# MLA attention rows: one exponential base per row, unnormalised weights, and 1/sum applied to the 64x256 output

## The chip, the core and the metric

The kernel runs on one core of one Trainium2 chip. The metric is device time in microseconds (us) for one execution, on the slowest core in use (here the only one). A core has five engines that run side by side, each with its own queue of instructions executed in order: PE (matrix products), DVE (vector work), ACT (functions of one operand, casts, copies), POOL (a second, slower vector engine) and SP (here it only issues memory transfers). They wait for each other through semaphores. Products land in PSUM, eight banks of 128 x 512 fp32; everything else lies in SBUF or in the chip's memory.

## The reference, cut to what matters

One decoder layer over 16 meta tokens and 1024 real tokens: RMSNorm, an input projection, three groups of heads side by side (stick-breaking attention, a Mamba-2 scan, MLA attention), an output projection, and a SwiGLU feed-forward block. The change concerns MLA, 8 heads with a query and key of 96 and a value of 64:

```
scale = 1 / sqrt(96)
s = einsum(q, k) * scale                       # causal, 128 queries at a time
p = softmax(where(mask, s, -1e30), axis=-1)    # over at most 1040 keys
o = einsum(p, v)
```

## The kernel before, in words

Tokens lie feature-major (features on partitions). A product of fp32 accuracy is made of three passes on numbers split into a high and a low part (`whi`, `wlo`, `hnh`, `hnl`, `mhi`, `mlo`, `ph`, `pl`): high x high, low x high, high x low. `load_w` brings a 512 KB weight tile to `wraw` (one buffer), ACT casts it to `whi`, POOL makes `wlo` (two buffers each). `dense_fm` (L126) runs the three passes (L135 to L137) into one of two PSUM banks `d_ps`, which a callback then empties.

Program order gives each instruction a priority; the framework then lists, engine by engine and before anything runs, what stands where, so that products of a later part fill the turns in which attention waits. On the chip each engine keeps that fixed order.

The MLA stage runs over heads c = 0 to 7 (`mla_head`), and in a head over j = 0 to 3, a pair of blocks of 128 queries (i = 2j and 2j + 1). For each block `mla_row` works through one to three chunks of keys (`key_chunks`: one chunk for i = 0, 1, 2, two for i = 3 to 6, three for i = 7; so 112 chunks, 64 rows, 32 pairs in the stage). Per chunk: PE computes scores into one of three PSUM banks `sc_ps` (L901 to L903, and the causal mask by L906), DVE takes the chunk's maximum (L908) and turns it into a bias (L909), and ACT exponentiates from PSUM into `pr` with that bias and a sum beside it (L910). As each chunk has its own base, the chunks are afterwards brought to one: DVE takes the least bias (L918), ACT exponentiates the differences (L919), DVE forms the row's sum and a factor for each chunk (L920 to L923; L915 for a row of one chunk), and DVE multiplies the whole row by it (L926; in the last two heads POOL takes chunks 1 and 2).

`weighted_values` then transposes the rows by PE into PSUM (`ptm`, `ptg`, L310 to L321), ACT casts (`ph`, L305), DVE subtracts (`pl`, L306), PE multiplies with the values (`pv`, L295 to L299), ACT and DVE add the two halves of the result (`half` L329, `oT` L331: 64 partitions x 256 queries), and ACT issues the store to memory (`s_omla`, L337). The same function serves the stick-breaking heads.

The filling work beside MLA is first the gate's projection (`gate_units`: loads `gy` by SP, L475; `gy` times the gate by POOL, L479; result `go` by DVE, L481; 1/rms of the tokens at its end, `rc` and `dg`), then the first rows of the output projection (`out_rows`: loads `raw` from `s_osb` and `s_ossm`, L966; sums into `hT`, L986). After the stage comes `OutGroup`, the rest of the output projection (operands by L1012, L1015, L1018), which reads `s_omla` back (L1059).

Of the kernel before, what the change touches and what calls it, by code (L numbers as in the profile page):

```python
# [11 lines left out]
F32 = mybir.dt.float32  # L12
# [3 lines left out]
AF = mybir.ActivationFunctionType  # L16
ALU = mybir.AluOpType
# [6 lines left out]
SEQ = 1024  # L24
# [35 lines left out]
def tile_hybrid_block(ctx: ExitStack, tc: tile.TileContext, a: dict):  # L60
# [11 lines left out]
    # ------------------------------------------------------------------ pools  # L72
# [43 lines left out]
    # ------------------------------------------------------------- primitives  # L116
# [24 lines left out]
    def col_rsqrt(r, x, tmp):  # L141
        """r = x^-1/2: a seed within 4% from the float's bits, 0x5f3759df - (bits >> 1), then Newton."""
        ri, xi = r.bitcast(I32), x.bitcast(I32)
        dve.tensor_scalar(ri, xi, 1, None, ALU.arith_shift_right)
        dve.tensor_scalar(ri, ri, -1, 0x5F3759DF, ALU.mult, ALU.add)
        for _ in range(3):
            dve.tensor_tensor(tmp, r, r, op=ALU.mult)
            dve.scalar_tensor_tensor(tmp, x, -0.5, tmp, ALU.mult, ALU.mult)
            dve.scalar_tensor_tensor(r, tmp, 1.5, r, ALU.add, ALU.mult)

    def token_rstd(cols, ps, squares, blocks, width, bufs=1):
        """1/rms of each token as columns [token in block, block]: squares are feature-major
        tiles whose sum over partitions and tiles is the token's sum of squares."""
# [20 lines left out]
    def spread(diag, row, r, blocks, t0, wide=None, bufs=2):  # L174
        """row[:, t - t0] = r of token t, on every partition."""
# [24 lines left out]
    # ---------------------------------------------------- phase 0: hn^T hi/lo  # L200
# [10 lines left out]
    # tiles of tags that the second head pair needs later: raw weights, squares  # L211
# [23 lines left out]
    def first_operands(i):  # L235
        """gain * x of the chunk's tokens, not yet over their rms, as products' operands"""
# [120 lines left out]
    # ------- phase 1: stick-breaking attention; convolution and step sizes beside it  # L357
    def step_sizes():
# [14 lines left out]
        # dt = softplus(dt_raw + bias), token-major; log decay and its sum within each chunk  # L373
# [10 lines left out]
        # log1p(u) = 2 s (1 + s^2/3 + s^4/5 + ...), s = u / (2 + u) <= 1/3  # L384
# [16 lines left out]
        # exact three-way bfloat16 split of the head-major running sum  # L401
# [42 lines left out]
    def add_squares(u, tile_, c0, n):  # L444
        """squares of the tile's chunk onto the token's sums so far, in grow"""
# [11 lines left out]
    def latent_units(w, dst, mov, chunks, blocks):  # L457
        """a latent projection to memory; 1/rms of its tokens as columns [token in block, block]"""
# [11 lines left out]
    def gate_units():  # L470
        """s_ossm = y silu(z), and 1/rms of its tokens as columns"""
# [15 lines left out]
        # two units share the early tokens' turn: the last tokens' y comes last  # L487
# [8 lines left out]
    def sb_values(g, w, blocks, r=None, banks=None):  # L496
        """token-major values of head pairs 2g, 2g+1"""
# [54 lines left out]
    # the first projections take the operands before 1/rms is known and scale their results  # L552
# [89 lines left out]
    # ------------- phase 2: SSD; beside it MLA's operands and the gate's projection  # L642
    def spread_row(row, r, blocks, chunks):
        for c0, m in chunks:
# [3 lines left out]
            act.copy(row[:, c0 : c0 + m], ps[:, :m])  # L648
# [6 lines left out]
    with ExitStack() as st:  # L655
# [121 lines left out]
        def latent(src, nt, n, gain, r, blocks, chunks):  # L777
            """(c * gain) hi/lo tiles, and 1/rms of each token as a row"""
# [13 lines left out]
            spread_row(row, r, blocks, chunks)  # L792
# [11 lines left out]
        # shared rotated key  # L804
# [24 lines left out]
        cq_mov, cq_row = latent(s_cq, 3, SEQ, gq, cq_r, real, CH_REAL)  # L829
# [34 lines left out]
    scale = 1.0 / math.sqrt(96.0)  # L864
    with ExitStack() as st:
# [22 lines left out]
        def mla_row(proj, i, late):  # L888
# [7 lines left out]
            # columns: 0-2 -scale * chunk max, 3 the least of them, 4-6 sums, 7-9 factors  # L896
            sm = mr.tile([128, 12], F32, tag="sm", bufs=6, name="sm")
            for x, (c0, n) in enumerate(chunks):
# [5 lines left out]
                if last:  # L904
# [3 lines left out]
                dve.tensor_reduce(sm[:, x : x + 1], ps[:, :n], AX.X, ALU.max)  # L908
                dve.tensor_scalar(sm[:, x : x + 1], sm[:, x : x + 1], -scale, None, ALU.mult)  # L909
                act.activation(  # L910
                    pr[:, c0 : c0 + n], ps[:, :n], AF.Exp, scale=scale, bias=sm[:, x : x + 1],
                    accum_out=sm[:, 4 + x : 5 + x],
                )
            if nch == 1:
                dve.reciprocal(sm[:, 7:8], sm[:, 4:5])  # L915
            else:
                # chunk factor exp(chunk max - row max) / row sum
                dve.tensor_reduce(sm[:, 3:4], sm[:, 0:nch], AX.X, ALU.min)  # L918
                act.activation(sm[:, 7 : 7 + nch], sm[:, 0:nch], AF.Exp, scale=-1.0, bias=sm[:, 3:4])  # L919
                dve.tensor_tensor(sm[:, 4 : 4 + nch], sm[:, 4 : 4 + nch], sm[:, 7 : 7 + nch], op=ALU.mult)  # L920
                dve.tensor_reduce(sm[:, 10:11], sm[:, 4 : 4 + nch], AX.X, ALU.add)
                dve.reciprocal(sm[:, 10:11], sm[:, 10:11])
                dve.tensor_scalar(sm[:, 7 : 7 + nch], sm[:, 7 : 7 + nch], sm[:, 10:11], None, ALU.mult)  # L923
            for x, (c0, n) in enumerate(chunks):
                n = min(n, n_all - c0)
                (pool if late and x in (1, 2) else dve).tensor_scalar(pr[:, c0 : c0 + n], pr[:, c0 : c0 + n], sm[:, 7 + x : 8 + x], None, ALU.mult)  # L926
            return pr

        def mla_head(c):
# [16 lines left out]
        # ------------- phase 3: the out projection; its first 512 rows beside MLA  # L946
# [14 lines left out]
        def out_rows(src, k0, nk, weights):  # L961
            """hT += 128 nk rows of w_out"""
# [61 lines left out]
    # ue lies where the values of the heads before the last two were  # L1024
# [667 lines left out]
```

## Time and profile before

| | |
|---|---|
| time, median of 3 runs | 1904.66 us (1904.15 to 1905.05) |
| span of the profiled execution, first to last instruction | 1903.1 us |
| mean granted PE clock over the span | 0.970 |
| stick-breaking stage, first score product to last store of `oT` | 81.6 to 533.7 us |
| MLA stage, first score product to last store of `oT` | 716.4 to 1100.1 us |

The profiled execution's span is 1.56 us below the median of the timed runs; the rest lies around the first and last instruction. A row of the profile names line, engine, operation, output and inputs, their shapes, and then times. "Busy" of PE is modelled for pipelined products, so that a PE shown fully busy may still have small gaps.

### The profile page before, as it was taken

The numbers are of one execution on the slowest core, as the hardware profiler recorded it, in microseconds if no ns is written. First come the engines' busy times: TensorE is split into PE (matmuls) and PEld (weight loads), VectorE is DVE, ScalarE is ACT, GpSimd is POOL, SyncE is SP. The second block draws the span as 40 slices with busy tenths as digits, with TensorE's granted clock in tenths as the row PEclk, the third lists the DMA queues.
The fourth block names the chain that finished last, engine by engine and source line by source line (L and its number), as shares of the span: only waits on it lengthen the run. The fifth ranks groups of instructions, "written<-read, shape, count | busy, mean of one in ns | idle before, by whom it ended". The sixth has DMA issues, their size and how long they took to land.

```text
span 1903.1 us, 27593 instructions
## 1 busy us (share of the span) xinstructions
PE 1763.0 (93%) x9788; PEld 1503.1 (79%) x9788; DVE 1489.8 (78%) x2472; ACT 890.1 (47%) x1993; POOL 892.1 (47%) x787
## 2 busy tenths in 40 slices
PE   8899999999999898998999988889999999889997
PEld 7778888888997687997778766768888888667787
DVE  8889679899756766778787889987667766899955
ACT  6555544555557657666444344432232223333333
POOL 3434224244345567455322357653244333678782
PEclk9899999999999999998999999899999999999998
DMA  4212112111254455334421323122222224723102
GB/s 150 60 46 69 53 47 70 35 58 62 74 150 146 149 167 159 97 103 121 148 65 37 139 68 111 45 89 73 80 89 87 78 72 143 278 77 113 54 1 89
DMA packets 102474, 178.42 MB, mean 94 GB/s; under 512 B 12208, under 2 KB 65168, under 8 KB 102336
## 3 DMA queue, kind: packets, MB, share of 16 engines
q1 hardware_dynamic: 82944, 161.10, 26.3%
q10 hardware_dynamic: 19392, 15.56, 2.8%
q8 instruction: 77, 1.26, 0.3%
q14 instruction: 61, 0.50, 0.1%
HBM read 125.15 MB, written 51.47 MB: 93 GB/s over the span
## 4 chain that ended last, share of the span: by engine, by line
PE 56%; DVE 25%; issue 7%; ACT 5%; POOL 3%; DMA 3%; SPq 0%; ACTq 0%; DVEq 0%; POOLq 0%
PE b_ps L1265 6%; PE b_ps L1267 6%; PE b_ps L1266 6%; PE d_ps L135 5%; PE d_ps L136 5%; PE d_ps L137 5%; DVE cacc L434 2%; DVE raw L1015 2%; PE pv L298 2%; DVE cm L615 2%; DVE op L1012 2%; PE pv L299 1%; PE b_ps L1466 1%; PE b_ps L1468 1%; PE b_ps L1467 1%
## 5 line engine op out<-in xcount | busy, mean ns | idle before, releaser
L135 PE MATMUL d_ps<-hnh,whi 128*128 128x384 f32 (+5 forms) x744 | 250.8, 337 | 8.1 <-DVE KS L541 5.3
L137 PE MATMUL d_ps<-hnl,whi 128*128 128x384 f32 (+5 forms) x744 | 249.7, 336 | 0.0
L136 PE MATMUL d_ps<-hnh,wlo 128*128 128x384 f32 (+5 forms) x744 | 248.4, 334 | 0.9 <-POOL cm L600 0.9
L1012 POOL TENSOR_TENSOR op<-raw,op 128x512 fp32r<-128x512 f32 x113 | 171.8, 1550 | 75.5 <-ACT op L1011 68.7
L124 POOL TENSOR_TENSOR wlo<-wraw,whi 128x1024 fp32r<-128x1024 f32 (+1 forms) x51 | 127.6, 2503 | 108.5 <-ACT whi L122 93.0
L135 PEld LDWEIGHTS d_ps<-hnh,whi 128*128 128x128 f32 (+1 forms) x744 | 143.0, 192 | 12.9 <-issue 3.8
L136 PEld LDWEIGHTS d_ps<-hnh,wlo 128*128 128x128 f32 (+1 forms) x744 | 142.5, 192 | 3.5 <-POOL cm L600 1.1
L137 PEld LDWEIGHTS d_ps<-hnl,whi 128*128 128x128 f32 (+1 forms) x744 | 142.9, 192 | 2.5
L1011 ACT CAST op<-raw 128x512 fp32r<-128x512 f32 x149 | 84.9, 618 | 117.7 <-PE d_ps L1468 50.4
L1265 PE MATMUL b_ps<-T,wh 128*128 128x512 f32 x352 | 138.4, 394 | 1.2 <-ACT T L1011 1.2
L1267 PE MATMUL b_ps<-T,wh 128*128 128x512 f32 x352 | 137.6, 392 | 0.0
L1266 PE MATMUL b_ps<-T,wl 128*128 128x512 f32 x352 | 137.1, 390 | 0.5 <-POOL wl L1012 0.5
L306 DVE TENSOR_TENSOR pl<-ptg,ph 128x512 fp32r<-128x512 f32 (+1 forms) x160 | 99.9, 627 | 40.0 <-ACT ph L305 39.3
L1012 POOL TENSOR_TENSOR wlo<-raw,whi 128x1024 fp32r<-128x1024 f32 (+1 forms) x22 | 52.9, 2402 | 149.2 <-ACT whi L1011 149.2
L615 DVE TENSOR_TENSOR_SCAN cm<-cm,zcol 128x144 f32<-128x144 f32 (+3 forms) x64 | 98.8, 1544 | 18.0 <-ACT cm L613 17.6
L298 PE MATMUL pv<-ph,V 128*128 128x256 f32 (+1 forms) x320 | 102.1, 325 | 7.1 <-DVE oT L331 4.2
L305 ACT CAST ph<-ptg 128x512 fp32r<-128x512 f32 (+1 forms) x160 | 86.1, 544 | 40.1 <-PE ptg L321 28.4
L1015 DVE TENSOR_TENSOR raw<-raw 128x512 f32<-128x512 f32 x58 | 70.5, 1221 | 40.5 <-DMA raw<-in_w_gate_dram 34.9
L1012 POOL TENSOR_TENSOR wl<-raw,wh 128x512 fp32r<-128x512 f32 x46 | 70.8, 1548 | 61.9 <-ACT wh L1011 61.9
L299 PE MATMUL pv<-pl,V 128*64 128x256 f32 (+1 forms) x320 | 89.0, 292 | 11.3 <-DVE pl L306 10.0
L1018 DVE TENSOR_TENSOR hF<-hF,b_ps 128x512 f32<-128x512 f32 (+1 forms) x96 | 58.8, 634 | 38.3 <-PE b_ps L1532 18.5
L298 PEld LDWEIGHTS pv<-ph,V 128*128 128x128 f32 (+1 forms) x320 | 60.8, 190 | 35.2 <-issue 14.9
(443 smaller groups left out, 5646.4 us busy)
## 6 DMA issues: line engine op xcount, KB each, us to landing
raw<-in_w_gate_dram SPq DMA_DIRECT2D x22, 512.0 KB, 3.6
raw<-in_w_up_dram SPq DMA_DIRECT2D x22, 512.0 KB, 4.3
s_hid<-gs SPq DMA_DIRECT2D x44, 256.0 KB, 2.0
raw<-in_w_down_dram SPq DMA_DIRECT2D x22, 512.0 KB, 4.7
raw<-s_hid SPq DMA_DIRECT2D x22, 512.0 KB, 5.4
wraw<-in_w_xbc_dram SPq DMA_DIRECT2D x12, 512.0 KB, 3.6
wraw<-in_w_o_dram SPq DMA_DIRECT2D x10, 512.0 KB, 3.6
s_xs<-csig SPq DMA_DIRECT2D x24, 192.0 KB, 1.9
```

Source lines behind the costliest of these rows:

```text
L124: pool.tensor_tensor(lo[:, :cols], raw[:, :cols], f32(hi[:, :cols]), op=ALU.subtract)
L135: pe.matmul(ps[:m, :n], wh, mh, start=(kt == 0), stop=False)
L136: pe.matmul(ps[:m, :n], wl, mh, start=False, stop=False)
L137: pe.matmul(ps[:m, :n], wh, ml, start=False, stop=(kt == nkt - 1))
L298: pe.matmul(out[:, :256], V[:kk, blk, hh, :], ph[:kk, c : c + 256], start=st, stop=False)
L299: pe.matmul(out[:64, :256], V[:kk, blk, hh, 0:64], pl[:kk, c : c + 256], start=False, stop=False)
L615: dve.tensor_tensor_scan(rev, rev, zcol.to_broadcast([128, n_all]), 1.0, ALU.mult, ALU.add)
L1012: eng.tensor_tensor(lo, value, f32(hi), op=ALU.subtract)
L1015: dve.tensor_tensor(out, x, y, op=ALU.subtract)
L1265: pe.matmul(banks[j], hi[:, ks], UH[u][k], start=start and k == 0, stop=False, skip_group_check=skip)
L1266: pe.matmul(banks[j], lo[:, ks], UH[u][k], start=False, stop=False, skip_group_check=skip)
L1267: pe.matmul(banks[j], hi[:, ks], UL[u][k], start=False, stop=stop and k == 3, skip_group_check=skip)
```

## The change

The factor 1/sqrt(96) moves from the exponentials into the row by which the queries' latent is scaled (`latent` and `spread_row` get a `scale`). In `mla_row` all chunks' negated maxima are taken first, their least is the bias of every chunk's exponential, and the row stays unnormalised. Its sum goes to a column of a new tile `inv`. For each pair DVE takes the reciprocal, SP stores the 256 numbers to memory (`s_inv`) and loads them back on 64 partitions (`fac`, 64 x 256), and in `weighted_values` POOL multiplies `oT` by them; the store of `oT` is then issued by SP and no longer by ACT. POOL's part in the last two heads' rows is gone.

```diff
+    s_inv = dram.tile([MLA_HEADS, NQ // 2, 256], F32, name="s_inv")
...
-    def weighted_values(tp, pvp, work, j, rows, V, hh, dram_out):
+    def weighted_values(tp, pvp, work, j, rows, V, hh, dram_out, factors=None):
...
-        act.dma_start(dram_out[:, 256 * j : 256 * (j + 1)], oT)
+        if factors is None:
+            act.dma_start(dram_out[:, 256 * j : 256 * (j + 1)], oT)
+        else:
+            pool.tensor_tensor(oT, oT, factors, op=ALU.mult)
+            sp.dma_start(dram_out[:, 256 * j : 256 * (j + 1)], oT)
...
-            act.copy(row[:, c0 : c0 + m], ps[:, :m])
+            act.activation(row[:, c0 : c0 + m], ps[:, :m], AF.Copy, scale=scale)
...
-        cq_mov, cq_row = latent(s_cq, 3, SEQ, gq, cq_r, real, CH_REAL)
+        cq_mov, cq_row = latent(s_cq, 3, SEQ, gq, cq_r, real, CH_REAL, 1.0 / math.sqrt(96.0))
...
-                dve.tensor_reduce(sm[:, x : x + 1], ps[:, :n], AX.X, ALU.max)
-                dve.tensor_scalar(sm[:, x : x + 1], sm[:, x : x + 1], -scale, None, ALU.mult)
-                act.activation(
-                    pr[:, c0 : c0 + n], ps[:, :n], AF.Exp, scale=scale, bias=sm[:, x : x + 1],
-                    accum_out=sm[:, 4 + x : 5 + x],
-                )
-            if nch == 1:
-                dve.reciprocal(sm[:, 7:8], sm[:, 4:5])
-            else:
-                dve.tensor_reduce(sm[:, 3:4], sm[:, 0:nch], AX.X, ALU.min)
-                act.activation(sm[:, 7 : 7 + nch], sm[:, 0:nch], AF.Exp, scale=-1.0, bias=sm[:, 3:4])
-                dve.tensor_tensor(sm[:, 4 : 4 + nch], sm[:, 4 : 4 + nch], sm[:, 7 : 7 + nch], op=ALU.mult)
-                dve.tensor_reduce(sm[:, 10:11], sm[:, 4 : 4 + nch], AX.X, ALU.add)
-                dve.reciprocal(sm[:, 10:11], sm[:, 10:11])
-                dve.tensor_scalar(sm[:, 7 : 7 + nch], sm[:, 7 : 7 + nch], sm[:, 10:11], None, ALU.mult)
-            for x, (c0, n) in enumerate(chunks):
-                n = min(n, n_all - c0)
-                (pool if late and x in (1, 2) else dve).tensor_scalar(pr[:, c0 : c0 + n], pr[:, c0 : c0 + n], sm[:, 7 + x : 8 + x], None, ALU.mult)
+                dve.tensor_reduce(sm[:, x : x + 1], ps[:, :n], AX.X, ALU.max, negate=True)
+                banks.append((ps, c0, n))
+            bias = sm[:, 0:1]
+            if nch > 1:
+                bias = sm[:, 3:4]
+                dve.tensor_reduce(bias, sm[:, 0:nch], AX.X, ALU.min)
+            for x, (ps, c0, n) in enumerate(banks):
+                acc = total if nch == 1 else sm[:, 4 + x : 5 + x]
+                act.activation(pr[:, c0 : c0 + n], ps[:, :n], AF.Exp, bias=bias, accum_out=acc)
+            if nch > 1:
+                dve.tensor_reduce(total, sm[:, 4 : 4 + nch], AX.X, ALU.add)
...
-                rows = [mla_row(proj, 2 * j + e, c >= 6) for e in range(2)]
-                weighted_values(tp, pvp, mr, j, rows, V, h, s_omla[p, 64 * h : 64 * (h + 1)])
+                inv = mr.tile([128, 2], F32, tag="inv", bufs=4, name="inv")
+                rows = [mla_row(proj, 2 * j + e, inv[:, e : e + 1]) for e in range(2)]
+                dve.reciprocal(inv, inv)
+                sp.dma_start(s_inv[c, j].rearrange("(e p) -> p e", e=2), inv)
+                factors = mr.tile([64, 256], F32, tag="fac", bufs=3, name="fac")
+                sp.dma_start(factors, s_inv[c, j].partition_broadcast(64))
+                weighted_values(tp, pvp, mr, j, rows, V, h, s_omla[p, 64 * h : 64 * (h + 1)], factors)
```

Line numbers after the change are about six higher. The order of every engine is the same as before up to the MLA stage, and again from the feed-forward block on; between the two the list is made anew. First place, DVE at the end of the fourth head, before: the rows around the last block of that head (three chunks, so `128x3`).

```order
L306 TENSOR_TENSOR pl<-ptm,ph 16x256
L306 TENSOR_TENSOR pl<-ptg,ph 128x512
L920 TENSOR_TENSOR sm<-sm 128x3
L921 TENSOR_REDUCE sm<-sm 128x1
L922 RECIPROCAL sm<-sm 128x1
L923 TENSOR_SCALAR sm<-sm 128x3
L306 TENSOR_TENSOR pl<-ptg,ph 128x512
L926 TENSOR_SCALAR pr<-pr,sm 128x272
L926 TENSOR_SCALAR pr<-pr,sm 128x384 x2
L908 TENSOR_REDUCE sm<-sc_ps 128x1
```

And DVE at the same block of the fourth head in the changed kernel (L915 is the chunk's maximum, L920 the least of them, L925 the row's sum, L308 is `pl`, L487 is `go`).

```order
L308 TENSOR_TENSOR pl<-ptm,ph 16x256
L915 TENSOR_REDUCE sm<-sc_ps 128x1 x2
L487 TENSOR_TENSOR go<-d_ps,gy 128x256
L920 TENSOR_REDUCE sm<-sm 128x1
L308 TENSOR_TENSOR pl<-ptg,ph 128x512 x2
L925 TENSOR_REDUCE inv<-sm 128x1
L915 TENSOR_REDUCE sm<-sc_ps 128x1
L308 TENSOR_TENSOR pl<-ptg,ph 128x384
L915 TENSOR_REDUCE sm<-sc_ps 128x1
L920 TENSOR_REDUCE sm<-sm 128x1
```

Between the reading of scores and the `pl` that feeds the products, the row's chain L920 to L926 has left the queue; two small reductions stand in its place.

Second place, SP where the filling work turns from the gate's projection to the output projection, before: the last of the four loads of `raw` from `s_osb`, without which no product of `out_rows` starts (`st` are loads of the next head's queries and keys).

```order
L966 DMA raw<-s_osb 128x1024
L482 DMA s_ossm<-go 128x256
L880 DMA st<-s_qn 64x1024
L880 DMA st<-s_qr 16x1024 x2
L966 DMA raw<-s_osb 128x1024
L880 DMA st<-s_kn 64x1040
L880 DMA st<-s_krot 32x1040
L966 DMA raw<-s_osb 128x1024
```

And SP at the same place of the changed kernel, from the third to the fourth of these loads (L970).

```order
L970 DMA raw<-s_osb 128x1024
L938 DMA s_inv<-inv 128x2x1
L885 DMA st<-s_qn 64x1024
L885 DMA st<-s_qr 16x1024
L940 DMA fac<-s_inv 64x256
L885 DMA st<-s_qr 16x1024
L938 DMA s_inv<-inv 128x2x1
L885 DMA st<-s_kn 64x1040
L343 DMA s_omla<-oT 64x256
L940 DMA fac<-s_inv 64x256
L885 DMA st<-s_krot 32x1040
L970 DMA raw<-s_osb 128x1024
```

Five transfers of the new chain now stand between the third and the fourth load; each `fac` waits for the landing of the `s_inv` ahead of it, and `s_omla` for POOL.

More of the change, by code (lines that the diff above doesn't have):

```diff
@@ L640, in tile_hybrid_block, with spread_row @@
     real = [(128 * b, 128) for b in range(NQ)]
-    def spread_row(row, r, blocks, chunks):
+    def spread_row(row, r, blocks, chunks, scale=1.0):
         for c0, m in chunks:
@@ L775, in row_tile, with latent @@
             return la.tile([128, T], F32, tag="lraw", bufs=4, name=name)
-        def latent(src, nt, n, gain, r, blocks, chunks):
+        def latent(src, nt, n, gain, r, blocks, chunks, scale=1.0):
             H, L = [], []
@@ L791, in latent @@
             row = la.tile([128, T], F32, tag="lrow", bufs=1, name="lrow")
-            spread_row(row, r, blocks, chunks)
+            spread_row(row, r, blocks, chunks, scale)
             return (lambda kt, c0, m: (H[kt][:, c0 : c0 + m], L[kt][:, c0 : c0 + m])), row
@@ L886, in mla_load, with mla_row @@
             return out
-        def mla_row(proj, i, late):
+        def mla_row(proj, i, total):
             QH, QL, KH, KL = proj
@@ L895, in mla_row @@
             nch = len(chunks)
[L897 removed]
+            sm = mr.tile([128, 8], F32, tag="sm", bufs=6, name="sm")
+            banks = []
             for x, (c0, n) in enumerate(chunks):
```

1 line of the change is left out of this document (removed).

## The prediction

> **What bounds the kernel now.** First the page: the span, the busy shares, and the chain that ended last by engine.
>
> ```profile
> span 1903.1 us, 27593 instructions
> PE 1763.0 (93%) x9788; PEld 1503.1 (79%) x9788; DVE 1489.8 (78%) x2472; ACT 890.1 (47%) x1993; POOL 892.1 (47%) x787
> PE 56%; DVE 25%; issue 7%; ACT 5%; POOL 3%; DMA 3%; SPq 0%; ACTq 0%; DVEq 0%; POOLq 0%
> ```
>
> PE is the bound, DVE the next. The change adds no product and removes none, so it can only give time where PE waits or runs at a lower clock. Next the windows of the MLA stage, cut where PE is full and where it isn't, then the whole stage and the one behind it. Columns: length, busy time of each engine (instructions), granted PE clock, DMA share, GB/s.
>
> ```profile
> core 0: us, PE busy (x) PEld busy (x) DVE busy (x) ACT busy (x) POOL busy (x), PEclk, DMA share, GB/s
> 716.00:750.00 34.00, 29.64 (x170) 26.60 (x171) 21.21 (x68) 22.66 (x60) 26.51 (x24) 0.90 0.59 162
> 750.00:850.00 100.00, 99.24 (x672) 91.36 (x671) 76.74 (x223) 67.14 (x172) 53.65 (x57) 1.00 0.38 108
> 850.00:910.00 60.00, 49.15 (x309) 42.95 (x309) 50.05 (x141) 37.21 (x97) 31.51 (x34) 0.89 0.37 109
> 910.00:980.00 70.00, 70.00 (x379) 57.55 (x378) 54.13 (x145) 33.44 (x83) 17.41 (x15) 1.00 0.34 110
> 980.00:1000.00 20.00, 16.99 (x90) 13.48 (x89) 19.26 (x36) 7.83 (x15) 7.04 (x7) 0.91 0.37 126
> 1000.00:1070.00 70.00, 70.00 (x392) 57.80 (x392) 56.32 (x156) 33.86 (x94) 22.90 (x26) 1.00 0.17 47
> 1070.00:1085.00 15.00, 12.23 (x57) 8.57 (x56) 13.33 (x25) 4.71 (x11) 7.13 (x6) 1.00 0.81 314
> ...
> 716.00:1102.00 386.00, 364.25 (x2147) 312.17 (x2148) 300.82 (x803) 210.45 (x535) 168.67 (x171) 0.97 0.35 106
> ...
> 1102.00:1204.00 102.00, 83.99 (x346) 64.99 (x346) 96.34 (x132) 46.93 (x81) 68.17 (x43) 0.92 0.26 88
> ```
>
> For 240 of 386 us (750:850, 910:980, 1000:1070) PE is full, and a lighter DVE gives nothing there. PE idles 60 − 49.15 = 10.9 us in 850:910, 3.0 in 980:1000, 2.8 in 1070:1085: 16.7 us in three places, where DVE is 83%, 96% and 89% busy. The 4.4 us of 716:750 lie at the start, with a DMA share of 0.59 and DVE busy 21 of 34: no DVE place. Who PE waited for in the stage (total, times, longest):
>
> ```profile
> PE pv L299 <- DVE pl L306: 7.1, 5, 2.6
> PE pv L298 <- ACT ph L305: 2.7, 2, 2.4
> PE d_ps L135 <- DVE go L481: 2.3, 4, 1.0
> PE sc_ps L901 <- ACT pr L910: 2.2, 2, 1.7
> PE d_ps L135 <- DVE hT L986: 1.7, 3, 0.9
> ...
> PE ptm L310 <- DVE pr L926: 1.5, 2, 1.2
> ```
>
> The largest, `pl`, is a DVE instruction that stands in order behind the row's chain. The timelines of the three engines at that place say why it was late:
>
> ```profile
> 881.45 4.71 POOL L884 TENSOR_TENSOR mlo<-st,mhi 96x1040 fp32r<-96x1040 f32 x2
> ...
> 884.30 2.85 DVE L923 TENSOR_SCALAR sm<-sm 128x3 f32<-128x3 f32 x1
> ...
> 887.65 0.47 PE L299 MATMUL pv<-pl,V 128*64 128x256 f32 x1 [2.57 <-DVE pl L306]
> ```
>
> A DVE instruction on three numbers a partition took 2.85 us, most of it beside POOL's `mlo` (to 886.16); `pl` came behind it, and PE waited 2.57 us.
>
> **What is removed.** The groups of the stage that the change takes from DVE, ACT and POOL (count | busy us, mean ns):
>
> ```profile
> L926 DVE TENSOR_SCALAR pr<-pr,sm 128x400 f32<-128x400 f32 (+5 forms) x100 | 47.6, 505 | 1.4
> L923 DVE TENSOR_SCALAR sm<-sm 128x2 f32<-128x2 f32 (+1 forms) x40 | 29.7, 743 | 0.8
> L920 DVE TENSOR_TENSOR sm<-sm 128x2 f32<-128x2 f32 (+1 forms) x40 | 16.4, 410 | 9.6 <-ACT sm L919 9.1
> L909 DVE TENSOR_SCALAR sm<-sm 128x1 f32<-128x1 f32 x112 | 15.4, 141 | 0.5
> L922 DVE RECIPROCAL sm<-sm 128x1 f32<-128x1 f32 x40 | 6.3, 157 | 0.7
> L915 DVE RECIPROCAL sm<-sm 128x1 f32<-128x1 f32 x24 | 3.6, 153 | 6.8 <-ACT pr L910 6.8
> ...
> L919 ACT ACTIVATE sm<-sm 128x2 f32<-128x2 f32 (+1 forms) x40 | 11.6, 294 | 10.6 <-DVE sm L918 10.5
> ...
> L926 POOL TENSOR_SCALAR pr<-pr,sm 128x384 f32<-128x384 f32 (+2 forms) x12 | 17.0, 1423 | 27.4 <-DVE sm L923 13.4 <-PE sc_ps L906 6.3 <-ACT sm L919 3.9
> ```
>
> DVE loses 47.6 + 29.7 + 16.4 + 15.4 + 6.3 + 3.6 = 119.0 us and gets 32 reciprocals of `inv` at L922's 157 ns, 5.0: 114 of its 300.8 us go. The other reductions stay, one for one. ACT loses 11.6 us and the issue of 32 stores. Off the path all that is worth nothing; what counts is how much of the 16.7 us it frees. `pl`, `ptm <- pr` and the wait of scores for ACT (itself held by the bias from DVE) hang on the chain; `go`, `hT` and part of `ph` do not. In the rows above that is 7.1 + 1.5 + 2.2 = 10.8 of 17.5, about two thirds. **Term A: 2/3 of 16.7 = −11.1 us** (none to all: 0 to −16.7; once `pl` is early, `ph` from ACT is late next).
>
> In two of these windows the clock is 0.89 and 0.91: 0.11 x 60 + 0.09 x 20 = 8.4 us of full-speed work lost there, and none in the full windows beside them. I let it go with the stalls in the same share. **Term B: −5.6 us** (0 to −8.4).
>
> A rule speaks against B. The Trainium skill, "TensorE: Matmul & The Clock Gate", section "HAM oscillation — how this bites in real kernels", has the clock fall when PE is idle for more than about 3.4 us. The longest wait quoted is 2.6 us, in a window that still shows 0.89, so the trace disagrees as far as single waits go; by the rule B would be 0.
>
> **What is added, and where it lies.** Prices from the nearest rows: POOL on 256 columns; stores and a small load (KB each, median us to landing); SP's longest wait; the last two `raw` loads at the turn of the filling work; the last `oT`, and DVE's wait behind it.
>
> ```profile
> L479 POOL TENSOR_TENSOR gy<-gy,gs 128x256 f32<-128x256 f32 x8 | 6.0, 756 | 0.0
> ...
> s_omla<-oT ACTq DMA_DIRECT2D x32, 64.0 KB, 2.0
> ...
> s_vsb<-vs ACTq DMA_DIRECT2D x2, 16.0 KB, 1.4
> ...
> dtb<-in_dt_bias_dram SPq DMA_DIRECT2D x1, 0.1 KB, 5.8
> ...
> SPq L120 <- POOL wlo L124: 83.2, 10, 15.5
> ...
> 885.46 0.42 SPq L966 DMA_DIRECT2D raw<-s_osb  x1
> ...
> 887.30 0.42 SPq L966 DMA_DIRECT2D raw<-s_osb  x1
> ...
> 1099.66 0.42 DVE L331 TENSOR_TENSOR oT<-pv,half 64x256 f32<-64x256 f32 x1 [0.19 <-ACT half L329]
> ...
> 1107.29 0.69 DVE L986 TENSOR_TENSOR hT<-hT,d_ps 128x512 f32<-128x512 f32 x1 [3.98 <-PE d_ps L137]
> ```
>
> *POOL:* 32 products of 64x256. No row has 64 partitions; half the 756 ns to twice it bounds them, and I take 756 as the columns are equal: 24.2 us for the 17.0 that go, in a stage where POOL works 168.7 of 386. The multiplication waits for `fac`, and behind it on POOL stand `wlo`, `mlo` and `gy`; SP already waits up to 15.5 us for POOL at `wraw` without PE showing a wait for `wlo`, so a few us are covered. Without that cover each late `wlo` would stop PE.
>
> *The round trip:* a store of 4-byte pieces and a spread load. No row shows such pieces; 1.4 and 5.8 us bound a landing, and I take 2.0, the store from the same place in the same stage. `fac` is wanted only when the pair's products are done. What waits is SP: each `fac` holds the queue for one landing, and at the turn two stand between the third and the fourth `raw`, which were 1.8 us apart. That is 2 x 2.0 = 4.0 us later (2.8 to 11.6), and the products of `out_rows` need all four. The attention's own products cover part. **Term C: +3 us** (0 to 11.6).
>
> *The end:* the last store waits for POOL's 0.76 us, and two loads of `w_o` are listed behind it that were issued before. DVE stood idle 3.98 us there and is then 96.3 of 102 us busy, so half is covered. **Term D: +1.5 us** (0 to 4).
>
> *The score banks:* a row's chunks now stay in PSUM until the row's least is known, at most one L908 and one L918 longer. There are three banks; two waits for them are in the rows (2.2 us), and the list was made with the longer hold. Twice those rows at worst, +2.2; I take 0. The `scale` goes into an ACT copy that runs anyhow: 0.
>
> **Sum**, against the profiled execution: 1903.1 − 11.1 − 5.6 + 3 + 1.5 = 1890.9; the median lies 1.56 above that span: **1892.5**, told as 1892.
>
> **The rivals.**
> (1) *More than two thirds:* all of A and B, the 4.4 us of the start and its clock (0.10 x 34 = 3.4), nothing added: 1904.7 − 32.9 = 1872. For it: DVE falls to half its time. Against: the start is a DMA place.
> (2) *The clock stays:* A comes, B does not: 1904.7 − 11.1 + 4.5 = 1898. For it: 716:750 shows 0.90 with DVE mostly free, so the clock falls from other causes too; against it, the full windows at 1.00. By the rule above it would be this one.
> (3) *No change:* PE's fixed list meets new late spots (`ph` from ACT, `go` behind POOL) that eat what `pl` gave: A a third, B nothing, C and D as above: 1904.7 − 5.6 + 4.5 = 1903.6.
> (4) *Slower:* SP at the turn. With landings at 5.8 us, the two `fac` there and the one ahead of the third load hold the queue 17.4 us, at a place without filling products, and PE goes to a half clock behind such a gap: some 4 us more. Then 1904.7 − 16.7 + 17.4 + 4 + 1.5 = 1911. It decides from landings of about 5 us; for it, 4-byte pieces are in no row; against it, the stores' 1.4 and 2.0.
> (5) *The change not doing what it says* would be `fac` ending the stage pair by pair, POOL always the last. That would show as PE waiting for `oT`; its time is that of (4).
>
> **How the numbers follow.** A measurement tells about 0.2% from no change, 3.8 us, so faster is below 1900.9 and slower above 1908.5. The forecast (1880 to 1897) has 0.50, (1) 0.08, (2) 0.12, (3) 0.15, (4) and (5) 0.15. Faster 0.70, same 0.15, slower 0.15. The range goes from (1) to just short of slower, 1873 to 1908, and leaves out the slow case and the edge of (1), under 0.2.
>
> **What the changed profile would show.** DVE busy near 187 us in the MLA stage, the stage near 374 us long; no PE wait on `pl` above 1 us; clock 0.95 or more at the turn; `s_inv` and `fac` landing in about 2 us each; POOL's multiplications near 0.76 us. Wrong is the forecast if PE waits at the first `out_rows` product for `raw` (C), if `pl` still holds PE (A), if clocks dip with short waits gone (B), or if DVE's work behind the stage starts more than 4 us after the last attention product (D).

## The result, and the profile after

The changed kernel takes 2037.17 us (median of 4 runs, 2031.94 to 2041.51) where the kernel before takes 1904.86 us (4 runs, 1904.15 to 1906.17): a ratio of 1.0685, 95% interval 1.0668 to 1.0703. It is 6.9% slower; 1892 us had been forecast. The MLA stage, from its first score product near 716 us, now has its last `oT` at 1222.3 us instead of 1099.66.

The page of the changed kernel: span, busy time (share) and count by engine, DMA packets, and the chain that ended last.

```profile
span 2030.2 us, 27377 instructions
PE 1801.9 (89%) x9788; PEld 1534.6 (76%) x9788; DVE 1394.7 (69%) x2148; ACT 881.9 (43%) x1953; POOL 896.9 (44%) x807
DMA packets 113738, 180.54 MB, mean 89 GB/s; under 512 B 21425, under 2 KB 76433, under 8 KB 113601
PE 46%; DVE 23%; DMA 14%; issue 6%; ACT 6%; POOL 4%; SPq 1%; ACTq 0%; DVEq 0%; POOLq 0%
```

DVE's busy time has fallen by 95 us in the span, nearly all of it in this stage (114 had been worked out), and it bought nothing: transfers went from 3% of the chain to 14%. The windows of the stage (length, busy time by engine, granted PE clock, DMA share, GB/s) show PE no longer full, and the clock down:

```profile
750.00:850.00 100.00, 84.69 (x510) 77.62 (x511) 36.56 (x96) 54.38 (x136) 48.56 (x55) 0.86 0.62 89
850.00:950.00 100.00, 77.26 (x424) 68.50 (x422) 33.32 (x90) 41.73 (x103) 39.91 (x46) 0.77 0.50 80
950.00:1050.00 100.00, 73.17 (x383) 59.40 (x384) 43.87 (x101) 38.37 (x92) 30.69 (x31) 0.84 0.43 106
```

Who SP's queue and PE waited for in the stage (total, times, longest):

```profile
SPq L940 <- DMA s_inv<-inv: 289.9, 32, 11.9
SPq L938 <- DVE inv L937: 31.0, 13, 8.6
...
PE d_ps L136 <- DVE go L487: 28.0, 5, 10.4
PE pv L300 <- DVE oT L333: 22.4, 4, 9.7
PE d_ps L136 <- ACT raw L972: 13.7, 1, 13.7
```

And the landing of the new store (KB each, median us from issue to landing; 8.4 at the least and 14.1 at the most):

```profile
s_inv<-inv SPq DMA_DIRECT2D x32, 1.0 KB, 10.0
```

A 1 KB store takes 10.0 us to land in the median of the 32 pairs, and SP, which issues in order, stands for it 289.9 us in total. One case followed through, in the timelines of SP, POOL, DVE and PE (start, duration; in brackets the idle time before and who ended it):

```profile
788.71 0.54 SPq L938 DMA_DIRECT2D s_inv<-inv  x1
...
800.30 0.45 SPq L940 DMA_DIRECT2D fac<-s_inv  x1
800.85 0.53 SPq L481 DMA_DIRECT2D gy<-s_y  x1
...
805.77 0.99 POOL L485 TENSOR_TENSOR gy<-gy,gs 128x384 f32<-128x384 f32 x1 [16.32 <-DMA gy<-s_y]
...
806.80 0.56 DVE L487 TENSOR_TENSOR go<-d_ps,gy 128x384 f32<-128x384 f32 x1 [12.42 <-POOL gy L485]
...
807.41 0.58 PE L136 MATMUL d_ps<-hnh,whi 128*128 128x256 f32 x1 [10.36 <-DVE go L487]
```

The windows of PE's wait and of what comes after it:

```profile
796.73:807.41 10.68, 0.33 (x2) 0.01 (x1) 0.61 (x2) 0.02 (x1) 0.99 (x1) 0.72 0.50 104
807.41:815.00 7.59, 7.58 (x32) 6.65 (x32) 3.75 (x10) 4.84 (x13) 3.72 (x6) 0.50 0.03 2
```

The timeline is to be followed downwards. `fac` cannot be issued before the store of 788.71 has landed; the load of `gy` stands behind it and goes out at 800.85; POOL, DVE and PE wait in turn; and after PE's 10.36 us without work the next 7.6 us run at a clock of 0.50. In the kernel before, PE was busy 11.54 of the 12 us from 796 to 808.

### The profile page after: what moved, and what is told of

Its sections match the earlier page's. It is cut to its first block, busy times and chain, and to the rows that moved or that the text cites. A ratio compares the mean times of both kernels' runs of the same rounds, so it can differ in the third digit from the quotient of the medians.

```text
span 2030.2 us, 27377 instructions
## 1 busy us (share of the span) xinstructions
PE 1801.9 (89%) x9788; PEld 1534.6 (76%) x9788; DVE 1394.7 (69%) x2148; ACT 881.9 (43%) x1953; POOL 896.9 (44%) x807
## 4 chain that ended last, share of the span: by engine, by line
PE 46%; DVE 23%; DMA 14%; issue 6%; ACT 6%; POOL 4%; SPq 1%; ACTq 0%; DVEq 0%; POOLq 0%
PE b_ps L1269 6%; PE b_ps L1271 6%; PE b_ps L1270 6%; DMA s_inv<-inv 6%; PE d_ps L136 3%; PE d_ps L138 3%; PE d_ps L137 3%; DVE raw L1019 3%; DVE cacc L440 2%; DVE cm L621 2%; PE pv L300 2%; DMA gy<-s_y 1%; DVE op L1016 1%; DVE hT L1022 1%; PE b_ps L1472 1%
## 5 line engine op out<-in xcount | busy, mean ns | idle before, releaser
L308 DVE TENSOR_TENSOR pl<-ptg,ph 128x512 fp32r<-128x512 f32 (+1 forms) x160 | 99.9, 629 | 70.0 <-ACT ph L307 69.3
L300 PE MATMUL pv<-ph,V 128*128 128x256 f32 (+1 forms) x320 | 107.1, 339 | 26.6 <-DVE oT L333 26.5
L136 PE MATMUL d_ps<-raw,whi 128*128 128x512 f32 x160 | 68.6, 429 | 34.4 <-ACT raw L972 13.7
```

The costliest lines, as they stand in the source:

```text
L136: pe.matmul(ps[:m, :n], wh, mh, start=(kt == 0), stop=False)
L300: pe.matmul(out[:, :256], V[:kk, blk, hh, :], ph[:kk, c : c + 256], start=st, stop=False)
L308: dve.tensor_tensor(pl[:kk, :n], pt[:kk, :n], f32(ph[:kk, :n]), op=ALU.subtract)
```

## The experiments

Four theories stood after the result. **T1**: SP stands behind each landing, and loads behind it come late. **T2**: POOL's multiplication, which waits for `oT`, holds `wlo`, `mlo` and `gy` behind it. **T3**: the whole row's maximum holds score banks and makes exponentials late. **T4**: the small packets of the stores load the DMA engines. Each ratio below is to runs of the kernel before on the same chip, with its 95% interval; 0.001 of it is 1.9 us. Where dependences change, the framework lists the engines' orders anew, so a few microseconds between two variants can be order alone.

**e1: no wait for the store.** The factor comes from an input tensor, so it is not 1/sum.

```diff
-                sp.dma_start(factors, s_inv[c, j].partition_broadcast(64))
+                sp.dma_start(factors, a["w_ukv"][0, 0:256].partition_broadcast(64))
```

> The changed kernel, with the 32 stores of s_inv as they are, but the 64x256 factors loaded from a piece of an input tensor instead of s_inv: the factor is then not 1/sum, and the load waits for no store. T1 (SP stands in order behind each landing of s_inv, and the loads behind it reach PE late): SP's wait at the load of fac goes from 289.9 us to under 10, the gaps of PE close and the time is 1880 to 1910 us. T2 (POOL's multiplication, which waits for oT with wlo, mlo and gy queued behind it): nothing it waits for has gone but fac itself, 13.6 us of POOL's waits; above 2000. T3 (the whole row's maximum, score banks held longer): unchanged, about 2037. T4 (the small packets of the stores load the DMA engines): unchanged, above 2000, since the stores still run.

Measured: 1984.09 us, ratio 1.0414 (1.0396 to 1.0433), outside the range of each theory. SP's wait at that load has gone, and some 52 us with it, but 79 us of loss remain: T1 is true and is the smaller part. With the stores still in, the transfers themselves are slow. Their median landings in e1 (the kernel before has 3.8 for `w_z`, 3.2 for `gy`, 3.6 for `s_kn`):

```profile
s_inv<-inv SPq DMA_DIRECT2D x32, 1.0 KB, 10.8
wraw<-in_w_z_dram SPq DMA_DIRECT2D x8, 512.0 KB, 12.0
gy<-s_y SPq DMA_DIRECT2D x16, 192.0 KB, 10.2
st<-s_kn SPq DMA_DIRECT2D x8, 260.0 KB, 11.3
```

Windows of e1 around one store, issued at 810.98 us, with seven loads and stores of 64 to 512 KB issued behind it up to 819.08:

```profile
810.00:812.00 2.00, 2.00 (x15) 1.96 (x14) 0.32 (x2) 1.25 (x5) 2.00 (x2) 1.00 0.31 89
812.00:814.00 2.00, 2.00 (x15) 1.89 (x14) 0.84 (x2) 0.62 (x3) 1.74 (x3) 1.00 2.31 33
814.00:816.00 2.00, 2.00 (x14) 1.68 (x13) 1.48 (x3) 1.07 (x3) 0.31 (x1) 1.00 0.02 10
816.00:818.00 2.00, 2.00 (x13) 1.62 (x11) 0.63 (x3) 1.97 (x6) 0.97 (x2) 1.00 1.37 47
818.00:820.00 2.00, 2.00 (x14) 1.63 (x14) 0.62 (x2) 1.01 (x4) 0.91 (x3) 1.00 0.55 25
820.00:822.00 2.00, 2.00 (x14) 2.00 (x13) 1.59 (x3) 0.72 (x2) 0.41 (x2) 1.00 0.31 27
822.00:824.00 2.00, 2.00 (x16) 1.84 (x15) 0.84 (x3) 1.73 (x2) 0.59 (x1) 1.00 0.98 365
```

The last two columns are read together: for ten microseconds 10 to 47 GB/s move although much is asked for, and then 365 GB/s at once. (A share above 1 comes from packets that last longer than the window and are counted where they start.) The trace's records of single packets say where the time lies. The store's own pieces start within 1.2 us, from 810.9 on, and none lasts more than 9 ns; the sixteen packets of 4 KB that start next, up to 813.4, last 3.0 to 8.7 us each. One store of 1 KB, quick to go out, holds up everything behind it.

**e2: two pieces instead of 256.** PE transposes the reciprocals, DVE copies them out, and the store is 2 x 512 B.

```diff
+                pv2 = tp.tile([128, 512], F32, tag="tp", name="ptv")
+                pe.transpose(pv2[:2, :128], inv, ident)
+                ivt = mr.tile([2, 128], F32, tag="ivt", bufs=1, name="ivt")
+                dve.tensor_copy(ivt, pv2[:2, :128])
-                sp.dma_start(s_inv[c, j].rearrange("(e p) -> p e", e=2), inv)
+                sp.dma_start(s_inv[c, j].rearrange("(e p) -> e p", e=2), ivt)
```

> The changed kernel, but PE transposes the 128x2 reciprocals into 2x128, DVE copies them out, and the store of s_inv is 2 pieces of 512 B instead of 256 of 4 B; the load of fac still waits for it. T1: the hold of SP scales with the landing; at 2 to 2.5 us a landing SP waits 32 x 2 to 2.5 = 64 to 80 us instead of 289.9, and of the 134 us above the kernel before about a quarter is left: 1900 to 1950 us. T4: gone with the pieces, 1880 to 1910 us, whatever the wait. T2, T3: above 2000. If the landing stays near 10 us with 2 pieces, the pieces are not the price of it, and T1 gives about 2037.

Measured: 1914.45 us, ratio 1.0056 (1.0041 to 1.0071). SP waits for these stores 27.3 us in 27 times instead of 289.9 in 32. With whole pieces and the same round trip, 120 of the 130 us have gone, which is T1's range and just above T4's; the run does not tell these two apart. T2 and T3 fall: POOL's multiplication and the row's maximum are in this kernel as in the changed one.

**e3: the load of the factor asked for late.** ACT writes one column of `fac` from `half` first, so the load comes after the pair's products; the stores are as they were.

```diff
+            act.copy(factors[:, 0:1], half[:, 0:1])
+            sp.dma_start(factors, src.partition_broadcast(64))
             pool.tensor_tensor(oT, oT, factors, op=ALU.mult)
```

> The changed kernel with the same stores and loads, but the load of fac is asked for after the pair's products (ACT first writes one column of fac from half, so the load cannot stand earlier); the store of s_inv has then landed for some microseconds. T1: SP's wait at the load of fac falls from 289.9 us to under 60, and the time to 1890 to 1940 us. T4: the traffic is the same, above 2000. T2: POOL waits for oT as before and now also 4 to 5 us a pair for fac to land: above 2030, more than the changed kernel if anything. T3: about 2037.

Measured: 1999.49 us, ratio 1.0497 (1.0480 to 1.0515). SP's wait at that load is down to 17.0 us, and still nearly 95 us are lost, more than e1's 79, since POOL now waits 149.0 us for `fac`. T1's 1890 to 1940 is missed, and so are T2's "above 2030" and T3's 2037; T4's "above 2000" is missed by half a microsecond.

**e4: the round trip alone, in the kernel before.** Two columns of the rows are copied, stored as 256 pieces and loaded back, and nobody reads them; all else is the kernel before.

```diff
+                inv = mr.tile([128, 2], F32, tag="inv", bufs=4, name="inv")
+                for e in range(2):
+                    dve.tensor_copy(inv[:, e : e + 1], rows[e][:, 0:1])
+                sp.dma_start(s_inv[c, j].rearrange("(e p) -> p e", e=2), inv)
+                factors = mr.tile([64, 256], F32, tag="fac", bufs=3, name="fac")
+                sp.dma_start(factors, s_inv[c, j].partition_broadcast(64))
```

> The kernel before, with nothing taken out, and for every pair DVE copies one column of each row into a 128x2 tile, SP stores it as 256 pieces of 4 B and loads it back on 64 partitions; nobody reads what is loaded (the round trip alone, without POOL's multiplication, the new row and the move of the store of oT). T1: SP waits about 290 us for the landings and the time is 1990 to 2060 us. T2, T3: 1900 to 1920, since neither the multiplication nor the row's maximum is in it. T4: as T1; this run does not tell T1 from T4.

Measured: 1998.76 us, ratio 1.0497 (1.0481 to 1.0513); SP waits 245.8 us for `s_inv`. The round trip by itself costs 95 us on the old rows. T2 and T3 are out for the bulk.

**e5: no stores.** As e1, and the store line is taken out.

```diff
-                sp.dma_start(s_inv[c, j].rearrange("(e p) -> p e", e=2), inv)
```

> As e1 (the factor from an input tensor, not 1/sum) and the 32 stores of s_inv left out as well; row, POOL's multiplication, the load of 64 KB per pair and the store of oT on SP all stay. Theory P (the 256 pieces of 4 B keep the whole DMA path from moving data for about 10 us each time, and T1's hold of SP is the smaller part): with the stores goes the rest of the loss, 1984 to 1885-1910 us, and loads that landed in 10 to 12 us in e1 (gy, wraw, st) land in 3 to 5 again. T1 alone: no wait of SP is left to remove, so 1970 to 1990 as e1. T2, T3: as e1.

Measured: 1912.79 us, ratio 1.0028 (1.0016 to 1.0039). The step from e1 is 1.0414 to 1.0028, 73.5 us, for 32 stores of 1 KB. Landings are back, in the answer for the stage:

```profile
gy<-s_y SPq DMA_DIRECT2D x14, 192.0 KB, 3.3
wraw<-in_w_z_dram SPq DMA_DIRECT2D x5, 512.0 KB, 3.8
```

**e6: the stores on another queue.** As e1, with `act.dma_start` for the store.

```diff
-                sp.dma_start(s_inv[c, j].rearrange("(e p) -> p e", e=2), inv)
+                act.dma_start(s_inv[c, j].rearrange("(e p) -> p e", e=2), inv)
```

> As e1 (the factor from an input tensor, not 1/sum), with the 32 stores of s_inv issued by ACT, on the queue that the kernel before used for oT. Theory Q (only what stands behind the small pieces on the same queue is held): SP's loads land in 3 to 5 us again and the time is 1890 to 1920 us. Theory P (the whole path is held, whatever the queue): loads on SP still land in 8 to 12 us after each store, and the time stays at 1960 to 2000 us.

Measured: 1979.40 us, ratio 1.0377 (1.0355 to 1.0399), as P says and not Q. The stores are on ACT's queue and SP's loads are about as late as in e1, in the answer for the stage (`gy` lands in 10.5 us and `st<-s_kn` in 11.4):

```profile
wraw<-in_w_z_dram SPq DMA_DIRECT2D x5, 512.0 KB, 9.0
...
s_inv<-inv ACTq DMA_DIRECT2D x32, 1.0 KB, 12.7
```

This fits the Trainium skill, "DMA: Bandwidth & Descriptors", section "Issuing engines are not separate DMA queues": transfers asked for by different engines run on the same 16 DMA engines.

**e7: pieces of 8 B.** As e1; each partition's two numbers lie side by side, so that 128 pieces fill the same 1 KB.

```diff
-                sp.dma_start(s_inv[c, j].rearrange("(e p) -> p e", e=2), inv)
+                sp.dma_start(s_inv[c, j].rearrange("(p e) -> p e", e=2), inv)
```

> As e1 (the factor from an input tensor, not 1/sum), but each store writes 128 pieces of 8 B instead of 256 of 4 B, to the same 1 KB of memory. If the price is per piece (10 us / 256 = 0.04 us each), the landing falls from 10.8 to about 6 us and half of the loss of e1 above the run without stores goes: about 1940 us. If it is per byte or per place, the landing stays at 10 to 11 us and the time at 1970 to 1990.

Measured: 1920.46 us, ratio 1.0062 (1.0038 to 1.0086), and a landing of 4.6 us (2.9 to 9.1). Half the pieces cost less than half: of e1's 73.5 us above e5, some 6 are left. The forecast of 1940 was too high.

**e8: pieces far apart.** As e1, with 512 B from one piece of 4 B to the next.

```diff
-    s_inv = dram.tile([MLA_HEADS, NQ // 2, 256], F32, name="s_inv")
+    s_inv = dram.tile([MLA_HEADS, NQ // 2, 256, 128], F32, name="s_inv")
...
-                sp.dma_start(s_inv[c, j].rearrange("(e p) -> p e", e=2), inv)
+                sp.dma_start(s_inv[c, j, :, 0].rearrange("(e p) -> p e", e=2), inv)
```

> As e1 (the factor from an input tensor, not 1/sum), but each of the 256 pieces of 4 B goes to a place of its own, 512 B from the next, so that no two share a line of memory. If the pieces wait for each other because they write into the same 1 KB, the landing falls to 2 to 4 us and the time to 1890 to 1920. If the price is per piece wherever it goes, the landing stays near 10 us and the time at 1970 to 1990.

Measured: 1910.51 us, ratio 1.0027 (1.0013 to 1.0041), as without any stores. **e12** has 64 B, and **e14** 32 B, in place of the 512 (`256, 16]` and `256, 8]` in the tile), one execution each:

> As e8 (256 pieces of 4 B, factor from an input tensor), with 64 B from one piece to the next instead of 512 B. If pieces only delay each other within 64 B, the landing stays at 1.7 to 3 us and the time near 1912; if they do within a longer stretch of memory (512 B, say), the landing lies between 3 and 11 us and the time between 1915 and 1985.

> As e12, with 32 B from piece to piece, so that two of the 256 pieces of 4 B lie in each 64 B. If two in 64 B already delay each other, the landing lies above the 1.6 us of e12, at 2 to 3 us (e7 has 8 in 64 B and 4.6 us, the changed kernel 16 and 10.0); if not, it is 1.6 us. The time 1905 to 1920 in both cases.

Measured: 1913.72 and 1916.78 us. The landings of e8:

```profile
s_inv<-inv SPq DMA_DIRECT2D x32, 1.0 KB, 1.7
```

of e12:

```profile
s_inv<-inv SPq DMA_DIRECT2D x32, 1.0 KB, 1.6
```

and of e14:

```profile
s_inv<-inv SPq DMA_DIRECT2D x32, 1.0 KB, 2.0
```

As many pieces, as small, to the same memory: at 512 or 64 B apart they land in 1.7 and 1.6 us, at 32 B in 2.0, packed in 10.8. So the price is that of small pieces lying close together. The runs fit a price for pieces that share 64 B (sixteen of them in the change, eight in e7, two in e14), but they don't fix that unit: nothing was tried between packed and 32 B, the step from 32 to 64 B is 0.4 us, and the stretch of memory that a store covers grows with the spacing (1 KB packed, 8 KB at 32 B, 16 KB at 64 B). Why it costs so much (one write waiting for the one before is the obvious reading) no run shows.

**e9: the store of `oT` on ACT again.** As e5, with one line changed.

```diff
             pool.tensor_tensor(oT, oT, factors, op=ALU.mult)
-            sp.dma_start(dram_out[:, 256 * j : 256 * (j + 1)], oT)
+            act.dma_start(dram_out[:, 256 * j : 256 * (j + 1)], oT)
```

> As e5 (factor from an input tensor, no stores of s_inv), with the store of oT issued by ACT as in the kernel before; POOL still multiplies. In e5 the last store of oT and, behind it on SP, the last two loads of w_o were issued at 1103.9 and 1104.5 us, and DVE, ACT and POOL then stood idle 6.5, 7.0 and 6.3 us for them. If the 8 us that e5 stands above the kernel before come from that place in SP's queue, this run is at 1900 to 1908 us and the loads of w_o are issued before the last store. If they come from the row (its exponentials wait for the whole row's maximum, 3.6 and 3.5 us waits of PE for ACT in e5), it stays at 1909 to 1915.

Measured: 1902.54 us, ratio 0.9975 (0.9965 to 0.9985), the first range, and the only run below the kernel before (its factor is not 1/sum). SP's timeline at the end of the stage in e5 (the second of the two stores goes out at 1104.0):

```profile
1092.41 12.01 SPq L343 DMA_DIRECT2D s_omla<-oT  x2
1104.47 1.07 SPq L1062 DMA_DIRECT2D raw<-in_w_o_dram  x2
```

and in e9:

```profile
1094.57 0.33 SPq L1062 DMA_DIRECT2D raw<-in_w_o_dram  x1
```

In e5 the loads of `w_o` stand behind the last store of `oT`, which waits for POOL; in e9 the last of them goes out at 1094.57, before that `oT` is made (1094.98).

**e10: the new row, normalised by DVE.** No round trip, no POOL, the store on ACT.

```diff
+                for e in range(2):
+                    n_all = META + 128 * (2 * j + e + 1)
+                    dve.tensor_scalar(rows[e][:, :n_all], rows[e][:, :n_all], inv[:, e : e + 1], None, ALU.mult)
+                weighted_values(tp, pvp, mr, j, rows, V, h, s_omla[p, 64 * h : 64 * (h + 1)])
```

> The change's row alone: one base for the row, and then, instead of the round trip, POOL's multiplication and the store on SP, DVE takes 1/sum of the pair and multiplies each row by it in one instruction (64 of them, in place of 100 on DVE and 12 on POOL); oT is stored by ACT. If the lighter chain frees PE as Terms A and B had it in part, 1890 to 1902 us. If what it frees is taken by later exponentials and by transposes that wait for the row's multiplication, 1902 to 1912.

Measured: 1921.59 us, ratio 1.0081 (1.0063 to 1.0098), above both ranges. PE's transposes wait 9.0 us in 5 times for these multiplications, which come in one piece a row and only when both rows have their sums; the last `oT` comes at 1115.63.

**e11: 1/sum by PE.** Each column of 1/sum, spread over 64 columns, is transposed into the free half of the pair's PSUM bank; DVE multiplies from there, ACT stores.

```diff
+            for e in range(2):
+                pe.transpose(out[:64, 256 + 128 * e : 384 + 128 * e], factors[:, e : e + 1].to_broadcast([128, 64]), ident)
...
+            dve.tensor_tensor(oT, oT, out[:64, 256:512], op=ALU.mult)
```

> The change without memory: PE transposes each column of 1/sum, spread over 64 columns, into the free half of the pair's own PSUM bank (2 transposes of 128x64 a pair), DVE multiplies oT by it from there (32 times 64x256 at about 0.42 us), and ACT stores oT. No transfer is added, and no engine waits for one. The gain of Terms A and B in full would be 1888 us plus 64 transposes at about 0.1 us, so 1890 to 1897. If the lighter row gives PE nothing, as e5 says, 1902 to 1912.

Measured: 1909.93 us, ratio 1.0014 (1.0001 to 1.0026): the whole change without a transfer, and no gain. The second range.

**e13: e2 with the store of `oT` on ACT**, the one line of e9.

> As e2 (PE transposes 1/sum, the store is 2 pieces of 512 B, the factor is loaded back from memory and is 1/sum), with the store of oT issued by ACT. If the wait of SP for the landing (27.3 us in 27 waits in e2) costs nothing on the path, the place of the last loads of w_o was all that e2 lost against e9, and the time is 1901 to 1906 us. If that wait still makes loads late, 1907 to 1914.

Measured: 1916.78 us, ratio 1.0053 (1.0037 to 1.0070), above both ranges: ACT's store won nothing here. SP's wait for the two pieces is 25.5 us, PE shows no long wait for loads, and its longest is 6.1 us for `pl`. At that place DVE and POOL show:

```profile
887.32 7.89 DVE L146 TENSOR_SCALAR rc<-rc 128x8 int32<-128x8 int32 x1
894.98 0.68 DVE L308 TENSOR_TENSOR pl<-ptg,ph 128x512 fp32r<-128x512 f32 x1
...
887.22 0.72 POOL L342 TENSOR_TENSOR oT<-oT,fac 64x256 f32<-64x256 f32 x1
887.91 4.69 POOL L889 TENSOR_TENSOR mlo<-st,mhi 96x1040 fp32r<-96x1040 f32 x2
892.54 0.20 POOL L326 MEMSET ph<- 128x128 f32 x1
892.71 2.33 POOL L977 TENSOR_TENSOR raw<-raw 128x1024 fp32r<-128x1024 f32 x1
```

An instruction on eight numbers a partition (its median in the span is 170 ns) takes 7.89 us, as long as POOL's row of work beside it, and `pl` and PE come behind. How the 15 us (by the ratios) between e13 and e9 divide among this, the transposes with their copies, and SP's waits was not tried; nor was a version found that computes 1/sum and beats the kernel before.

## Why the prediction was wrong

Taken away in the order of the runs, the loss of 0.0685 divides, by the ratios: 0.0271 (52 us) for SP's wait, from the change to e1; 0.0386 (74 us) for the packed pieces, e1 to e5; 0.0053 (10 us) for the store of `oT` on SP, e5 to e9; and −0.0025 (−5 us) left as the gain of the rest. These are steps in one order, not fixed prices. SP's wait is as long as it is because the packed landing is: with two whole pieces SP still waits for each landing, and all that is lost is some 11 us (e2). And the store of `oT` on SP, worth 10 us between e5 and e9, is worth nothing between e2 and e13.

**Term C (+3 us, 0 to 11.6) is the step that failed**, in three ways. Its price: "1.4 and 5.8 us bound a landing, and I take 2.0"; it landed in 10.0. By the term's own working that is 2 x 10.0 = 20 us and a sum near 1910, so the price alone does not make the 132 us. The rows taken as bounds held no store of 4-byte pieces, and the text said so and bounded all the same. Its place: the wait was counted at the turn of the filling work, "two stand between the third and the fourth `raw`", and SP stood in all 32 pairs, with `gy` and `w_z` behind it where only `raw` had been looked at. And its kind: a wait of SP was the only cost thought of, while the larger part, 74 us, is that the pieces slow the transfers behind them to a near stop (e1, e5), and not on their own queue alone, which e6 showed.

**Rival (4)** had the mechanism of the smaller part, SP held behind each landing, and the point where it decides ("from landings of about 5 us"): at 10.0 it did. Its 1911 us counted one place of the stage. That the stores hold up other transfers is in no term and no rival.

**Term A (−11.1 us)** was too large. e9 is the nearest run in which the new row stands and transfers are harmless. Its `pl` waits have gone from PE's largest (7.1 us before), and its last `oT` comes 4.7 us earlier, which agrees with the 4.8 us of its ratio. Windows of e9 at the three places of the sum:

```profile
850.00:910.00 60.00, 51.77 (x321) 46.35 (x319) 39.13 (x91) 35.18 (x89) 34.52 (x39) 0.86 0.44 131
...
980.00:1000.00 20.00, 18.82 (x108) 14.88 (x107) 16.36 (x29) 11.94 (x28) 12.20 (x8) 1.00 0.43 138
...
1070.00:1085.00 15.00, 14.85 (x78) 11.73 (x77) 13.61 (x29) 7.63 (x19) 3.58 (x4) 1.00 0.05 16
```

Of 16.7 us of idle PE 9.6 are left, nearly all (8.2) in 850:910. What is late next there was the question that the term left open; e9's PE waits, from the stage's start to 1250 us, answer it:

```profile
PE d_ps L180 <- DVE dg L179: 8.4, 2, 4.7
...
PE ptm L312 <- ACT pr L923: 4.9, 2, 4.1
```

Of the 8.4 us, 3.75 are in 850:910, at 894.47; the 4.7 lie behind the stage, at 1201. DVE and POOL show why `dg` was late in this window:

```profile
888.43 5.06 DVE L150 SCALAR_TENSOR_TENSOR rc<-rc 128x8 f32<-128x8 f32 x1
...
885.77 4.72 POOL L889 TENSOR_TENSOR mlo<-st,mhi 96x1040 fp32r<-96x1040 f32 x2
...
890.46 0.71 POOL L342 TENSOR_TENSOR oT<-oT,fac 64x256 f32<-64x256 f32 x1
891.14 2.33 POOL L972 TENSOR_TENSOR raw<-raw 128x1024 fp32r<-128x1024 f32 x1
```

The prediction had seen a 2.85 us instruction of the row "beside POOL's `mlo`" and counted it as the row's. By the rows it was the clash that cost, and with the row's chain gone it takes the next small DVE instruction, `rc`, from which `dg` is made: three of them last 2.31, 2.31 and 5.06 us in e9, and in e11 the same clash makes PE wait 6.2 us for `dg`. In this stage of the kernel before, 20 DVE instructions on at most 9 numbers a partition (reductions aside) last over 0.6 us, and POOL is at work for 96% or more of each, though it works only 168.7 of the 386 us. No run took POOL's work away to test it. The other wait, `pr`, comes from ACT's order and not from the row's maximum: the row's least was ready at 882.4, but ACT had stood 1.68 us for a load of `raw`, and from 882.34 on it cast `raw` and `mhi` and copied `half`, so that the exponentials began at 885.70. Late work on ACT is what rival (3) had looked for, in `ph`.

**Term B (−5.6 us)** came to nothing: the clock is 1.00 for 0.91 in 980:1000, 1.8 us gained, and 0.86 for 0.89 in 850:910, 1.8 us lost. Rival (2) was right on this. In 850:910 of e9 PE waits 4.07 us and, 4 us later, 3.75, and the clock between and behind them is 0.50; in the changed kernel a wait of 10.36 us is followed by a clock of 0.50. Both agree with the Trainium skill, "TensorE: Matmul & The Clock Gate", section "HAM oscillation — how this bites in real kernels", by which the clock falls after waits above 3.4 us and B would be 0. Shorter waits have the same effect in these traces, though: in the kernel before, the clock is 0.74 in 881.2:885.1, right behind a wait of 2.39 us, and 0.50 in 885.1:890, through the next wait of 2.57 us. So the 0.89 of the sum can come from waits too, and the two that are left in e9 are enough to keep it.

**Term D (+1.5 us, 0 to 4)** was about right at its place and missed the rest: the store on SP costs 10 us by e5 and e9. At the place itself DVE stands idle 6.50 us in e5 and 4.66 in e9, 1.8 us apart; most of the rest lies in the stage, which ends 7.7 us earlier in e9. How that divides, and how much of it is only the new order of the engines, was not tried.

**The small terms held.** POOL's multiplication takes 728 ns in the mean (756 taken), the score banks make PE wait 1.7 us for ACT in e9 and 3.5 in e5 (2.2 before, 0 more taken), and `pl` holds PE for 1.1 us in all in e5, though for 6.1 at once in e13. The profile's forecast "`s_inv` and `fac` landing in about 2 us each" was the line that failed first.

## What to carry to other kernels

A store of pieces of a few bytes that lie side by side in memory is no small transfer (10.8 us here for 1 KB in pieces of 4 B). Before a round trip through memory is priced like any other store, look at its pieces, and set them apart (64 B was enough here) or turn the data so that they are whole runs. A load that waits for a store on an in-order queue is charged to everything that stands behind it, in every iteration and not only at the place where the queue looks tight. And a small instruction that is slow beside another engine's long one tells of the clash: removing that instruction moves the wait to the next one.

## What was not expected of the hardware

- A store of 256 pieces of 4 B took 1.6 us to land with the pieces 64 B apart and 10.8 us with them packed into 1 KB (e12, e1), and while the packed ones were under way the transfers behind them stood nearly still (10 to 47 GB/s, then 365, in e1); SP's loads came late also when ACT had issued the stores (e6). The Trainium skill, "DMA: Bandwidth & Descriptors", section "Specifications", says that a piece under 512 B is read, modified and written back. Size alone is not what costs here: pieces of 4 B cost nothing that e8 could measure against e5.
- DVE instructions of 0.17 us took 5.06 and 7.89 us beside POOL. The Trainium skill, "SBUF — State Buffer", section "Who interferes with whom", describes a port pair that DVE and GpSimd (POOL here) share: whichever issues first has it for its whole instruction, and the other is blocked. The traces agree, with two `rc` of 2.31 us in e9 beside POOL instructions of about that length, and go further: a DVE instruction was held over several POOL instructions in a row, from 887.32 to 895.2 us in e13 and from 888.43 to 893.5 in e9, and not over one.
